# Reordering the pieces of the last tile in a row-wise infinity norm, and one tail store for two

## The chip, the cores and the metric

The kernel runs on one core of one Trainium2 chip. The metric is device time in microseconds; most executions agree within 0.3%. A trace's span runs from its first to its last instruction and is about 1.8 us shorter than the device time of the same execution.

## The reference

```python
x = np.random.randn(8192, 8192).astype(np.float32)     # 268 MB
out = np.linalg.norm(x, ord=np.inf, axis=1)            # max of |x| along each row
```

## The kernel before

Each of the 128 partitions handles 64 rows, two rows (16384 columns, 64 KB) to a tile, with three tile buffers. First come 24 bulk tiles, each one load of 8.39 MB and one VectorE reduce of 17.22 us. Then come 8 tail tiles, whose loads are cut into pieces (`TAIL`) so that VectorE can begin on a piece while the next one is still in flight. A maximum of each piece goes into `part`; one small reduce ("the merge") turns `part` into the results of the first 15 tail rows. The pieces of the last row are treated in another way: their partial maxima are written just behind the tile's data, so that the last reduce takes the last piece and all partial maxima in one instruction.

```python
TAIL = [
    [2944, 13440], [4096, 12288], [11520, 4864], [7680, 8704],
    [6528, 3328, 6528], [4864, 4096, 3328, 4096], [3968, 3584, 3328, 2944, 2560],
    [2432, 2176, 1920, 1664, 1536, 1280, 1152, 1024, 1152, 1024, 1024],
]                                     # reformatted: one list per tile
...
                if r < n_tail - 1:
                    absmax(part[:, r, k : k + 1], t[:, lo : lo + n])
                    if r == n_tail - 2 and k == count[r] - 1:
                        absmax(r_tail[:, : n_tail - 1], part[:])          # the merge
                        nc.scalar.dma_start(out=out_t[:, : n_tail - 1], ...)
                elif k < n_last - 1:
                    absmax(t[:, W + k : W + k + 1], t[:, lo : lo + n])
                else:
                    absmax(r_fin[:], t[:, lo : W + n_last - 1])           # the last reduce
    nc.sync.dma_start(out=out_t[:, n_tail - 1 :], in_=r_fin[:])
```

(Cuts are marked by dots. `absmax` is `reduce_max` with absolute values on VectorE; `nc.sync` and `nc.scalar` are the queues of SyncE, SP, and ScalarE, ACT.)

## Time and profile before

| | us |
|---|---|
| device time, median of 3 | 628.22 |
| span of the traced execution | 626.05 |
| last bulk load lands | 466.66 |
| last load of all lands | 622.90 |
| last reduce | 623.11 to 624.34 |
| last store | 624.37 to 625.78 |

How to read it: the last three rows follow one another. From the start of the last reduce on, nothing overlaps, so the reduce and the store count in full. Landings are read as the issue time of a load plus its time to landing.

Page of the kernel before: engine busy time with its share of the span, and the DMA queues with packets, MB and the share of the 16 DMA engines' time. q1 carries the loads, q10 the stores from ACT, q14 instruction fetches.

```profile
DVE 552.9 (88%) x64; POOL 0.2 (0%) x4
q1 hardware_dynamic: 8064, 268.44, 99.4%
q10 hardware_dynamic: 928, 0.03, 0.1%
q14 instruction: 2, 0.02, 0.0%
```

The load queue is busy all the time. VectorE (DVE) has 12% slack over the whole run, but that average hides the tail. The next view is the timeline of the kernel before from 605 us: start, duration, engine and line, with consecutive instructions of a kind merged.

```profile
603.36 11.64 DVE L139 TENSOR_REDUCE part<-t 128x1 f32<-128x2560 f32 x5
606.13 7.17 SPq L157 DMA_DIRECT2D t<-in_x_dram  x4
615.04 0.22 DVE L139 TENSOR_REDUCE r_tail<-part 128x15 f32<-128x60 f32 x1
615.17 7.91 DVE L139 TENSOR_REDUCE t<-t 128x1 f32<-128x1536 f32 x6
615.29 0.35 ACTq L169 DMA_DIRECT2D out_dram<-r_tail  x1
623.11 1.23 DVE L139 TENSOR_REDUCE r_fin<-t 128x1 f32<-128x1030 f32 x1
624.37 0.35 SPq L177 DMA_DIRECT2D out_dram<-r_fin  x1
```

The chain of waits of the same trace from 580 us: start, duration, what (pieces of 0.02 us left out).

```profile
556.05 40.57 DMA t<-in_x_dram
596.64 18.38 DVE part L139 x8
615.04 0.22 DVE r_tail L139
615.26 7.83 DVE t L139 x6
623.11 1.23 DVE r_fin L139
```

The chain leaves the loads at 596.6 us. From there to 624.34 us it stays on VectorE, which has no idle gap any more: the last landing at 622.90 is not on this chain at all, because VectorE was still 0.21 us behind when it came. The last load's own line among the DMA issues (KB, us from issue to landing; issued at 612.98) and the three stores' lines are:

```profile
t<-in_x_dram SPq DMA_DIRECT2D x1, 512.0 KB, 9.9
out_dram<-r_bulk ACTq DMA_DIRECT2D x1, 24.0 KB, 60.4
out_dram<-r_tail ACTq DMA_DIRECT2D x1, 7.5 KB, 5.4
out_dram<-r_fin SPq DMA_DIRECT2D x1, 0.5 KB, 1.4
```

### The profile page before, as it was taken

The numbers are of one execution on the slowest core, as the hardware profiler recorded it, in microseconds if no ns is written. First come the engines' busy times: TensorE is split into PE (matmuls) and PEld (weight loads), VectorE is DVE, ScalarE is ACT, GpSimd is POOL, SyncE is SP. The second block draws the span as 40 slices with busy tenths as digits, with TensorE's granted clock in tenths as the row PEclk, the third lists the DMA queues.
The fourth block names the chain that finished last, engine by engine and source line by source line (L and its number), as shares of the span: only waits on it lengthen the run. The fifth ranks groups of instructions, "written<-read, shape, count | busy, mean of one in ns | idle before, by whom it ended". The sixth has DMA issues, their size and how long they took to land.

```text
span 626.0 us, 199 instructions
## 1 busy us (share of the span) xinstructions
DVE 552.9 (88%) x64; POOL 0.2 (0%) x4
## 2 busy tenths in 40 slices
DVE  0588988889988889888898888988889999999998
POOL 0000000000000000000000000000000000000000
DMA  9999999999999999999999999999999999999997
GB/s 402 469 402 452 419 452 419 452 419 448 423 435 435 427 444 410 461 402 469 402 469 402 469 402 465 406 452 419 452 422 410 443 432 430 423 431 426 427 424 308
DMA packets 8994, 268.49 MB, mean 429 GB/s; under 512 B 1952, under 2 KB 1952, under 8 KB 3104
## 3 DMA queue, kind: packets, MB, share of 16 engines
q1 hardware_dynamic: 8064, 268.44, 99.4%
q10 hardware_dynamic: 928, 0.03, 0.1%
q14 instruction: 2, 0.02, 0.0%
HBM read 268.44 MB, written 0.03 MB: 429 GB/s over the span
## 4 chain that ended last, share of the span: by engine, by line
DMA 67%; DVE 29%; another core or an unknown queue 4%; SPq 0%; issue 0%
DMA t<-in_x_dram 67%; DVE r_bulk L139 22%; DVE part L139 5%; DVE t L139 1%; DVE r_fin L139 0%; SPq L157 0%; DVE r_tail L139 0%
## 5 line engine op out<-in xcount | busy, mean ns | idle before, releaser
L139 DVE TENSOR_REDUCE r_bulk<-t 128x2 f32<-128x16384 f32 x24 | 413.3, 17220 | 69.6 <-DMA t<-in_x_dram 69.6
L139 DVE TENSOR_REDUCE part<-t 128x1 f32<-128x8192 f32 (+18 forms) x31 | 130.4, 4274 | 0.8 <-DMA t<-in_x_dram 0.6
L139 DVE TENSOR_REDUCE t<-t 128x1 f32<-128x1152 f32 (+3 forms) x6 | 7.9, 1387 | 0.0
L139 DVE TENSOR_REDUCE r_fin<-t 128x1 f32<-128x1030 f32 x1 | 1.2, 1227 | 0.0
L136 DVE MEMSET part<- 128x60 f32 x1 | 0.1, 108 | 0.9 <-PEq L194 0.9
L139 DVE TENSOR_REDUCE r_tail<-part 128x15 f32<-128x60 f32 x1 | 0.2, 216 | 0.0
L194 POOL MEMSET const-uint8-127<- 128x1 uint8 x1 | 0.1, 102 | 0.0
L194 POOL MEMSET const-bfloat16-1.0<- 128x1 bf16 x1 | 0.1, 101 | 0.0
L194 POOL MEMSET const-float32-0.0<- 128x1 f32 x1 | 0.1, 98 | 0.2 <-issue 0.2
L194 POOL MEMSET const-float32-1.0<- 128x1 f32 x1 | 0.1, 98 | 0.0
## 6 DMA issues: line engine op xcount, KB each, us to landing
t<-in_x_dram SPq DMA_DIRECT2D x1, 6720.0 KB, 40.4
t<-in_x_dram SPq DMA_DIRECT2D x2, 3264.0 KB, 26.2
t<-in_x_dram SPq DMA_DIRECT2D x3, 2048.0 KB, 28.7
t<-in_x_dram SPq DMA_DIRECT2D x1, 6144.0 KB, 40.6
t<-in_x_dram SPq DMA_DIRECT2D x1, 5760.0 KB, 35.3
t<-in_x_dram SPq DMA_DIRECT2D x3, 1664.0 KB, 32.2
t<-in_x_dram SPq DMA_DIRECT2D x2, 2432.0 KB, 32.4
t<-in_x_dram SPq DMA_DIRECT2D x1, 4352.0 KB, 43.0
```

The source lines that it names most:

```text
L136: nc.vector.memset(part[:], 0.0)
L139: nc.vector.reduce_max(out=o, in_=i, axis=X, apply_absolute_value=True)
L194: nc = _bacc.Bacc("TRN2", target_bir_lowering=False, num_devices=1)
```

## The change

Its intent: shorten what follows the last landing. Both rows of the last tile now keep their partial maxima in the tile, each beside its last piece; the two last pieces are the last two loads, of 640 columns each. The merge of the other 14 rows needs nothing of the last tile any more, and one store writes all 16 tail rows. The other tail lists are cut anew.

```diff
 TAIL = [
-    [2944, 13440], [4096, 12288], [11520, 4864], [7680, 8704],
-    [6528, 3328, 6528], [4864, 4096, 3328, 4096], [3968, 3584, 3328, 2944, 2560],
-    [2432, 2176, 1920, 1664, 1536, 1280, 1152, 1024, 1152, 1024, 1024],
+    [9728, 6656], [5632, 10752], [9600, 6784], [9344, 7040],
+    [6784, 6528, 3072], [4736, 3072, 4224, 4352], [3968, 2432, 3072, 2944, 1792, 2176],
 ]
+LAST = (
+    [(0, w) for w in (2176, 2048, 1664, 1664)]
+    + [(1, w) for w in (1536, 1280, 1152, 1024, 896, 896, 768)]
+    + [(0, 640), (1, 640)]
+)
...
+    for j, (b, w) in enumerate(LAST):
+        final = left[b] == 0
+        to = slot[b] - w if final else at          # the last pieces go next to the partial maxima
+        frm = b * cols + col[b]
+        nc.sync.dma_start(out=t[:, to : to + w], in_=x_t[len(TAIL)][:, frm : frm + w])
+        if final:
+            absmax(r_tail[:, r : r + 1], t[:, to : slot[b] + parts_of[b]])
+        else:
+            absmax(t[:, k : k + 1], t[:, to : to + w])
+        if j == 0:
+            absmax(r_tail[:, : n_tail - B], part[:])
-    nc.sync.dma_start(out=out_t[:, n_tail - 1 :], in_=r_fin[:])
+    nc.sync.dma_start(out=out_t, in_=r_tail[:])
```

More of the change, by code (lines that the diff above doesn't have):

```diff
@@ L17 @@
 TAIL = [
-    [2944, 13440],
-    [4096, 12288],
-    [11520, 4864],
-    [7680, 8704],
-    [6528, 3328, 6528],
-    [4864, 4096, 3328, 4096],
-    [3968, 3584, 3328, 2944, 2560],
-    [2432, 2176, 1920, 1664, 1536, 1280, 1152, 1024, 1152, 1024, 1024],
-]
+    [9728, 6656],
+    [5632, 10752],
+    [9600, 6784],
+    [9344, 7040],
+    [6784, 6528, 3072],
+    [4736, 3072, 4224, 4352],
+    [3968, 2432, 3072, 2944, 1792, 2176],
+]
+LAST = (
[3 more added lines that the diff above has]
+)
 def segments(loads, cols):
@@ L107 @@
     W = B * cols
-    n_tail = B * len(TAIL)
+    n_tail = B * (len(TAIL) + 1)
     n_bulk_rows = rows // P - n_tail
@@ L123 @@
     segs = [segments(loads, cols) for loads in TAIL]
-    count = {}
-    for i, s in enumerate(segs):
-        for _, r, _, _ in s:
-            count[i * B + r] = count.get(i * B + r, 0) + 1
-    n_last = count[n_tail - 1]
-    k_max = max(count[r] for r in range(n_tail - 1))
-    assert n_last - 1 <= PAD
+    k_max = max(sum(r == b for _, r, _, _ in s) for s in segs for b in range(B))
+    parts_of = [sum(r == b for r, _ in LAST) - 1 for b in range(B)]
+    assert sum(parts_of) <= PAD
     r_bulk = outp.tile([P, A, G * B], F32)
     r_tail = outp.tile([P, n_tail], F32)
-    r_fin = outp.tile([P, 1], F32)
-    part = outp.tile([P, n_tail - 1, k_max], F32)
+    part = outp.tile([P, n_tail - B, k_max], F32)
     nc.vector.memset(part[:], 0.0)
@@ L149 @@
     nc.scalar.dma_start(out=out_b, in_=r_bulk[:])
-    seen = {}
     for i, loads in enumerate(TAIL):
@@ L154 @@
         todo = segs[i]
+        seen = [0] * B
         at = 0
@@ L159 @@
             for _, b, c, n in [s for s in todo if s[0] == j]:
-                r = i * B + b
-                k = seen.get(r, 0)
-                seen[r] = k + 1
-                lo = b * cols + c
-                if r < n_tail - 1:
-                    absmax(part[:, r, k : k + 1], t[:, lo : lo + n])
-                    if r == n_tail - 2 and k == count[r] - 1:
-                        absmax(r_tail[:, : n_tail - 1], part[:])
-                        nc.scalar.dma_start(
-                            out=out_t[:, : n_tail - 1], in_=r_tail[:, : n_tail - 1]
-                        )
-                elif k < n_last - 1:
-                    absmax(t[:, W + k : W + k + 1], t[:, lo : lo + n])
-                else:
-                    absmax(r_fin[:], t[:, lo : W + n_last - 1])
-    nc.sync.dma_start(out=out_t[:, n_tail - 1 :], in_=r_fin[:])
+                k, lo = seen[b], b * cols + c
+                absmax(part[:, i * B + b, k : k + 1], t[:, lo : lo + n])
+                seen[b] += 1
+    t = sbuf.tile([P, W + PAD], F32, tag="t")
+    left = parts_of[:]
+    col = [0] * B
+    at, slot = 0, {}
+    ends = [w for _, w in LAST[-B:]]
+    lo = W - sum(ends)
+    for b in range(B):
+        slot[b] = lo + ends[b]
+        lo = slot[b] + parts_of[b]
+    for j, (b, w) in enumerate(LAST):
[3 more added lines that the diff above has]
+        nc.sync.dma_start(out=t[:, to : to + w], in_=x_t[len(TAIL)][:, frm : frm + w])
+        col[b] += w
+        if final:
+            r = n_tail - B + b
+            absmax(r_tail[:, r : r + 1], t[:, to : slot[b] + parts_of[b]])
+        else:
+            left[b] -= 1
+            k = slot[b] + left[b]
+            absmax(t[:, k : k + 1], t[:, to : to + w])
+            at += w
+        if j == 0:
+            absmax(r_tail[:, : n_tail - B], part[:])
+    nc.sync.dma_start(out=out_t, in_=r_tail[:])
     nc.at_finalize(start_first_load_early)
```

## The prediction

> **What bounds the kernel now.** The load stream. The page gives q1 (the SP loads) 99.4% of the 16 DMA engines' span at 429 GB/s; successive landings give 19.34 us per 8.39 MB bulk tile, 434 GB/s. The Trainium skill ("DMA: Bandwidth & Descriptors", Specifications) gives 435 GB/s as the fabric ceiling; the trace agrees, so 268 MB cannot stream faster. VectorE is 88% busy, but starts the tail 17 us behind (bulk reduce of 17.22 us ending at 483.90) and catches up only at the end: in the timeline it works without a break of over 0.7 us from 483.8 to 624.34. The skill ("VectorE: DVE Perf Modes") says that the reduce has only its 1x mode; the trace agrees (8192 elements in 8.68 us, 1.04 ns each plus 0.14 us, of which 0.085 us overlaps the next one).
>
> Only the end is open to this change: the last load lands at 622.90, VectorE finishes the reduce before at 623.08, the final 1030-element reduce runs 623.11 to 624.34 (1.23 us), the 0.5 KB store 624.37 to 625.78, and the span ends at 626.05.
>
> **What changes.**
> - The last load and reduce shrink from 1024/1030 to 640/647 elements: about 0.82 us (the trace's 640-element form). Saves 0.40 us on the path.
> - The final reduce no longer depends on the reduce just before it: the 0.03 us hand-over becomes a 0.085 us overlap, and VectorE's lag behind the last landing, 0.21 us now, should be 0.05 to 0.1. Saves 0.1 us.
> - Loads in the tail: 31 to 34. From the intervals between landings I estimate 1.16 ns per column plus 0.065 us per load plus 0.04 us per further 2048 columns; this reproduces all 31 landings within 0.5 us cumulated. The new lists cost 0.28 us more.
> - The 7.5 KB ACT store amid the last loads (5.4 us to landing, 144 packets between the loads' packets; those loads take some 0.1 us more than the estimate) is gone. Saves 0.1 us.
> - The last store grows from 4 to 64 bytes per partition: packets of 60 bytes took 11 ns, of 4 bytes 9 ns, eight per engine. Costs 0.02 us.
> - Reduces in the tail: 39 to 42, each 0.06 us of overhead, 0.18 us. VectorE's idle time absorbs it. Stepping through the new list with these durations, it stays 0.02 to 0.25 us behind each landing in the last tile.
> - The reordered larger pieces move work about but save nothing: VectorE frees each buffer while over a tile is still in flight.
>
> **Sum.** The last load lands 0.2 us later (623.1), the last reduce ends 0.3 us earlier (about 624.0), and the store takes the same 1.4 us. I predict 627.9 us, 0.05% below 628.22; range 627.4 to 628.4. Faster by over 2%: 0.005; within 2%: 0.99; slower: 0.005.
>
> **What would show it.** Timeline: last reduce about 0.82 us, starting within 0.1 us of the last landing; last landing near 623.1; no ACT store after the bulk one; 64-byte store landing in about 1.4 us; q1 still above 99%.
>
> **What would make it wrong.** Two 8 KB instruction fetches share the DMA engines (one falls on a landing that is 0.3 us late); a third, or another placing, moves the end by 0.3 us. A destination at a 16-byte offset could slow the last load's writes. If the SP queue issues the small loads late, the stream starves. VectorE has almost no slack: an unforeseen wait of 0.3 us in the middle of the tail would appear in full.

## The result and the profile after

The median was 627.98 us (627.73 to 628.23, 6 runs) against 628.23 us before (628.11 to 629.08, 6 runs of the same comparison). The ratio was 0.9993, with a 95% interval of 0.9981 to 1.0006. Ratios here are the mean time of one kernel's fast runs over that of the other's in the same rounds, so they are not quite the ratios of the medians. By the 2% criterion the two are the same, and that interval alone can't tell the difference from zero.

The page of the kernel after, the lines that answer to those of before:

```profile
DVE 552.9 (88%) x67; POOL 0.2 (0%) x4
q1 hardware_dynamic: 8496, 268.45, 99.4%
q10 hardware_dynamic: 784, 0.02, 0.1%
q14 instruction: 2, 0.02, 0.0%
```

Its timeline from 604 us:

```profile
604.17 2.41 DVE L140 TENSOR_REDUCE part<-t 128x1 f32<-128x2176 f32 x1
606.48 8.55 SPq L179 DMA_DIRECT2D t<-in_x_dram  x5
606.61 0.21 DVE L140 TENSOR_REDUCE r_tail<-part 128x14 f32<-128x56 f32 x1
606.74 16.47 DVE L140 TENSOR_REDUCE t<-t 128x1 f32<-128x2176 f32 x11
623.13 1.55 DVE L140 TENSOR_REDUCE r_tail<-t 128x1 f32<-128x644 f32 x2
624.71 0.35 SPq L192 DMA_DIRECT2D out_dram<-r_tail  x1
```

The chain of waits of the kernel after, from 580 us (from 622.83 us on, where the last two reduces overlap, the view goes over to small pieces under other names; these are left out, as are pieces of 0.02 us):

```profile
553.77 35.14 DMA t<-in_x_dram
588.93 17.66 DVE part L140 x7
606.61 0.21 DVE r_tail L140
606.82 16.01 DVE t L140 x11
```

The last load (issued at 614.70) and the last store among the DMA issues, and, by form, the last reduce (the 1.23 us of the one before stand in its timeline above):

```profile
t<-in_x_dram SPq DMA_DIRECT2D x1, 320.0 KB, 8.9
out_dram<-r_tail SPq DMA_DIRECT2D x1, 8.0 KB, 1.4
```

```profile
L140 DVE TENSOR_REDUCE r_tail<-t 128x1 f32<-128x647 f32 x1 | 0.8, 816 | 0.0
```

The merge has moved from 615.0 to 606.6 us. The ACT store is gone from the end. The last reduce takes 0.82 us instead of 1.23, and the store of 8 KB takes 1.4 us like the one of 0.5 KB. But this one execution ended its span 0.35 us later than the traced one of before: its last bulk load had landed 0.31 us later (466.97), and its last load landed 156.64 us after that one, against 156.24 before. A single trace of each kernel therefore can't say what was won. What I need is a quantity that scatters less than the landings do. That quantity is the time from the last landing to the end of the last reduce: 1.44 us before, 1.07 us after.

### The profile page after: what moved, and what is told of

Read it like the earlier page. It is cut to its first block, busy times and chain, and to the rows that moved or that the text cites. A ratio compares the mean times of both kernels' runs of the same rounds, so it can differ in the third digit from the quotient of the medians.

```text
span 626.4 us, 204 instructions
## 1 busy us (share of the span) xinstructions
DVE 552.9 (88%) x67; POOL 0.2 (0%) x4
## 3 DMA queue, kind: packets, MB, share of 16 engines
q1 hardware_dynamic: 8496, 268.45, 99.4%
## 4 chain that ended last, share of the span: by engine, by line
DMA 63%; DVE 35%; issue 1%; another core or an unknown queue 0%; DVEq 0%
DMA t<-in_x_dram 63%; DVE r_bulk L140 24%; DVE part L140 8%; DVE t L140 3%; DVEq L220 0%; DVE r_tail L140 0%
## 5 line engine op out<-in xcount | busy, mean ns | idle before, releaser
L140 DVE TENSOR_REDUCE part<-t 128x1 f32<-128x8192 f32 (+20 forms) x28 | 121.6, 4410 | 0.9 <-DMA t<-in_x_dram 0.8
L140 DVE TENSOR_REDUCE t<-t 128x1 f32<-128x1664 f32 (+8 forms) x11 | 16.5, 1572 | 0.0
L140 DVE TENSOR_REDUCE r_tail<-t 128x1 f32<-128x644 f32 (+1 forms) x2 | 1.5, 814 | 0.0
```

Of the source, the lines that this page charges most:

```text
L140: nc.vector.reduce_max(out=o, in_=i, axis=X, apply_absolute_value=True)
```

## The experiments

Twelve kernels ran in three groups, each group on another chip and beside its own runs of the kernel before: e1 to e4 (kernel before: median 628.36, 9 runs), e5, e6, e7 and e9 (628.13, 9 runs), e8, e10, e11 and e12 (628.12, 9 runs). Each experiment has five timed runs and one trace. "Lag" is the time from the last landing to the start of the last reduce; "lag + last" is the time from the last landing to its end.

| kernel | last load after last bulk load, us | lag | last reduce | lag + last | median of time, us | ratio, 95% interval |
|---|---|---|---|---|---|---|
| before | 156.24 | 0.21 | 1.23 | 1.44 | 628.22 | |
| e9 before again | 156.34 | 0.21 | 1.23 | 1.43 | 628.27 | 1.0002 (0.9990, 1.0015) |
| after | 156.64 | 0.25 | 0.82 | 1.07 | 627.98 | 0.9993 (0.9981, 1.0006) |
| e1 after again | 156.13 | 0.24 | 0.82 | 1.05 | 627.89 | 0.9993 (0.9981, 1.0006) |
| e12 after, third | 156.49 | 0.25 | 0.81 | 1.07 | 627.79 | 0.9992 (0.9978, 1.0005) |
| e2 large pieces only | 156.15 | 0.22 | 1.23 | 1.44 | 628.12 | 0.9999 (0.9987, 1.0012) |
| e3 mid store | 156.46 | 0.19 | 0.82 | 1.01 | 627.92 | 0.9995 (0.9983, 1.0008) |
| e4 skip one reduce | 156.68 | 0.12 | 0.82 | 0.94 | 627.96 | 0.9992 (0.9979, 1.0006) |
| e5 small end, old order | 156.43 | 0.65 | 0.83 | 1.48 | 628.10 | 1.0001 (0.9989, 1.0014) |
| e10 e5 with early merge | 156.54 | 0.46 | 0.83 | 1.28 | 627.98 | 0.9997 (0.9984, 1.0009) |
| e6 coarse end | 156.35 | 0.09 | 2.29 | 2.38 | 629.00 | 1.0016 (1.0002, 1.0030) |
| e8 finer end | 156.48 | 0.53 | 0.55 | 1.09 | 627.92 | 0.9995 (0.9983, 1.0008) |
| e7 aligned end | 156.35 | 0.28 | 0.82 | 1.10 | 627.98 | 0.9996 (0.9984, 1.0009) |
| e11 two tiles | 156.61 | 0.16 | 0.81 | 0.98 | 627.78 | 0.9993 (0.9980, 1.0005) |

(The last bulk load's landing is taken as 0.02 us before the start of the reduce that waited for it.)

### Is there a gain at all? (e1, e9, e12)

The edit: none. e1 and e12 are the kernel after, e9 the kernel before.

> The changed kernel unaltered, for its scatter and a second trace. Theory A (the gain is real and comes from the smaller last reduce): 0.2 to 0.4 us under the kernel before in the mean, last reduce about 0.82 us, last load landing 156.5 us after the last bulk load (before: 156.24, first trace of the change: 156.64). Rival N (no gain, only scatter between runs): within 0.1 us of the kernel before.

> The kernel before, unaltered, for a second trace. Theory A: last landing to end of last reduce 1.44 us again, within 0.05; last landing 156.0 to 156.6 us after the last bulk landing, scatter from the place of the 8 KB instruction fetch. Rival N: this interval scatters as much as the totals do (some 0.5 us).

> The changed kernel unaltered beside the three others on this chip. Last landing to end of last reduce 1.07 us again, within 0.05; mean 0.2 to 0.4 us under the kernel before.

Lag + last came out at 1.05 and 1.07 us again, and at 1.43 us for the kernel before: it repeats within 0.02 us. The landing of the last load does not repeat: 156.13, 156.49 and 156.64 us in three traces of one and the same kernel. Over all groups, the 16 timed runs of the kernel after have a mean of 627.89 us and the 38 of the kernel before (with e9's five) 628.27 us. The difference is 0.39 us; from the scatter of these runs I work out a 95% interval of about 0.14 us to either side. It was 0.41, 0.45 and 0.49 us in the three comparisons taken separately. So the gain is real, though the interval of each single comparison includes no change at all, and it is 0.06%. A few long runs of the kernel before (up to 629.08 us) raise its mean: the medians of the two sets, 628.14 and 627.84 us, differ by 0.30 us.

The two traces e1 and after also show where much of the scatter arises. Both have one packet of the instruction queue q14 (8 KB) at 582.1 to 582.2 us. In both, the load of 4352 columns then lands: 5.25 us after its predecessor in e1, 5.71 us in the other. The neighbouring sizes suggest about 5.2 us (5.05 us was measured for 4224 columns). The timeline of VectorE alone around that time, first of the kernel after, then of e1:

```profile
570.97 12.85 DVE L140 TENSOR_REDUCE part<-t 128x1 f32<-128x4736 f32 x4
584.17 9.04 DVE L140 TENSOR_REDUCE part<-t 128x1 f32<-128x4352 f32 x2 [0.36 <-DMA t<-in_x_dram]
```

```profile
570.97 21.72 DVE L140 TENSOR_REDUCE part<-t 128x1 f32<-128x4736 f32 x6
```

In the kernel after VectorE waited 0.36 us for that landing, in e1 it did not wait. In six traces with these tail lists (after, e1, e3, e4, e7, e12) this interval was 5.71, 5.25, 5.57, 5.76, 5.50 and 5.62 us, so it differs by up to 0.5 us between runs of nearly the same program (5.34, 5.68 and 5.58 us in e2, e6 and e8, which share these lists). It holds nearly all the scatter of the last landing: without it, the three traces of the change have 150.93, 150.88 and 150.87 us from the last bulk landing to the last one.

The old lists have such a late load too, 4096 columns, in 5.18 us (before) and 5.28 us (e9). In e10, below, the packet comes later, and there this load takes 4.89 us. With 4.89 us for it in the kernel before, and 5.2 us for the 4352 columns in the change, the last load lands 155.95 and 155.96 us after the last bulk load before, and 156.13, 156.08 and 156.07 us in the change: 0.14 us later.

That the instruction packet is the cause is inferred. What speaks for it is that in e10 and e11, where the packet came at 610.1 and 606.9 us, the late load moved with it. But each trace has a second such packet, and the load around that one was never more than 0.1 us late, so a packet alone doesn't explain it.

### Do the larger pieces carry it? (e2)

```diff
 # the kernel before
-    [2944, 13440], ..., [3968, 3584, 3328, 2944, 2560],
+    [9728, 6656], ..., [3968, 2432, 3072, 2944, 1792, 2176],
     [2432, 2176, 1920, ..., 1152, 1024, 1024],
```

> The kernel before with the seven new larger tail lists; its last tile and its two tail stores are as before. Theory A (the gain comes from the last tile alone): no gain, the same as before or up to 0.2 us slower (one load and two reduces more). Rival B (the new larger pieces let VectorE catch up earlier and carry the gain): 0.2 us or more faster than before.

It is as slow as the kernel before (ratio 0.9999), with lag + last 1.44 us. The new lists for the seven earlier tiles gain nothing by themselves. In this trace VectorE waited 0.22 us for the first load of the last tile (at 606.2 us), and its lag at the end was 0.22 us all the same: what the earlier lists do doesn't reach the end of the old last tile.

### Does the removed store carry it? (e3)

```diff
 # the kernel after
             absmax(r_tail[:, : n_tail - B], part[:])
+            nc.scalar.dma_start(out=out_t[:, : n_tail - B], in_=r_tail[:, : n_tail - B])
-    nc.sync.dma_start(out=out_t, in_=r_tail[:])
+    nc.sync.dma_start(out=out_t[:, n_tail - B :], in_=r_tail[:, n_tail - B :])
```

> The changed kernel with the store of the 14 finished tail rows put back on the ACT queue amid the last loads, and the last store for two rows only. Theory A: the 144 small packets delay the last landing by about 0.1 us, so 0 to 0.1 us slower than the change, still under the kernel before. Rival C (the removed store is the gain): as slow as the kernel before, 0.25 us above the change.

Its median was 627.92 us, 0.03 us from e1's, and the last load landed 156.46 us after the last bulk load, amid the three traces of the change (156.13 to 156.64). The store amid the loads costs nothing that these runs resolve. Without the one late load (above) it is 150.89 us, against 150.87 to 150.93: no cost within 0.05 us. This still doesn't refute my 0.1 us, because e3 issues the store at 606.4 us, 9 us earlier than the kernel before does. In the one trace of e3 the last store took 1.72 us instead of 1.41 to 1.45; I can't say why.

### Is it just the smaller last piece? (e5)

This is the experiment that decides most. It makes the last reduce as small as the change does, with one line, and leaves everything else as before.

```diff
 # the kernel before
-    [2432, 2176, 1920, 1664, 1536, 1280, 1152, 1024, 1152, 1024, 1024],
+    [2432, 2176, 1920, 1664, 1536, 1280, 1152, 1024, 896, 896, 768, 640],
```

> The kernel before with one line changed: its last list ends 896, 896, 768, 640 in place of 1152, 1024, 1024, so the last reduce has 647 elements; row order, tail stores and all other lists as before. Theory A (the size of the last piece is the gain): from the last landing to the end of the last reduce 1.05 us as in the change (before: 1.44), last landing about 0.07 us later than before for one more load, total as fast as the change, 0.3 us under before. Rival R (the row order with both rows ending in the last two loads, or the single store, is needed): no faster than before.

It is not faster than the kernel before: ratio 1.0001. Lag + last was 1.48 us. The timeline of e5 from 615 us, and its last load (issued at 614.95) among the issues:

```profile
615.21 0.22 DVE L139 TENSOR_REDUCE r_tail<-part 128x15 f32<-128x60 f32 x1
615.34 8.37 DVE L139 TENSOR_REDUCE t<-t 128x1 f32<-128x1536 f32 x7
...
623.74 0.83 DVE L139 TENSOR_REDUCE r_fin<-t 128x1 f32<-128x647 f32 x1
```

```profile
t<-in_x_dram SPq DMA_DIRECT2D x1, 320.0 KB, 8.1
```

The last reduce takes 0.83 us as hoped. But it starts 0.65 us after its data landed (623.09), because VectorE is still at work on the pieces before. What the last reduce no longer does, VectorE has to do just before it, plus the overhead of one instruction more. Its chain of waits is that of the kernel before, on VectorE alone from 596.8 us. When an engine is behind, the end is the time of its last wait plus all its work since, and cutting that work into other pieces does not shorten it. So theory A, in the form in which I had written it for e5, is wrong: the small end alone is not enough, and rival R is right that something else of the change is needed. R's other half, the single store, is ruled out by e3, which keeps two stores and the whole gain in lag + last. The earlier lists are no candidate either: in e5 and in the kernel before, the first reduce of the last tile (606.31 and 606.14 us) starts 0.02 us after its landing, so the whole lag arises within that tile (see also e2). What is left is the last tile itself: its order, the sizes of its pieces and the place of the merge. No run separates these three; other sizes in the old order were not tried.

### What the new order buys (e10)

If e5 fails for VectorE's backlog, then taking work out of its last stretch must help. e10 is e5 with the merge before the last tile. The result is wrong (row 14's maximum isn't there yet), as the old order doesn't allow it.

```diff
 # e5
-                    if r == n_tail - 2 and k == count[r] - 1:
+                    if r == n_tail - 3 and k == count[r] - 1:
```

> Wrong result on purpose (row 14 of 16 is merged before its maxima are there): the small end in the old row order, e5, with the merge of partial maxima and its store moved from before the 1536-column piece (615 us) to before the last tile (606 us). In e5 the lag was 0.65 us and ate the whole gain. Theory B (what the new row order buys is an early merge, out of VectorE's last stretch): lag 0.35 to 0.4 us, last reduce 0.83 us, total 0.25 us under e5 and as fast as the change. Rival R2 (the lag in e5 has another cause, such as the hand-over to the last reduce): lag 0.55 us or more, total as e5.

The timeline of e10 from 606 us:

```profile
606.10 0.21 DVE L139 TENSOR_REDUCE r_tail<-part 128x15 f32<-128x60 f32 x1
...
611.53 3.95 DVE L139 TENSOR_REDUCE part<-t 128x1 f32<-128x1920 f32 x2 [0.17 <-DMA t<-in_x_dram]
615.39 8.37 DVE L139 TENSOR_REDUCE t<-t 128x1 f32<-128x1536 f32 x7
623.79 0.83 DVE L139 TENSOR_REDUCE r_fin<-t 128x1 f32<-128x647 f32 x1
```

The lag fell from 0.65 to 0.46 us, between my two figures. But the trace doesn't show that the early merge did it. The load for which VectorE waited 0.17 us at 611.5 us, 1920 columns, landed 2.85 us after its predecessor, against 2.28 us in e5 and in the kernel before: it was 0.57 us late, and an instruction packet came at 610.1 us, as the DMA view of e10 from 610 to 610.2 us shows:

```profile
q14 instruction: 1, 0.01, 9.7%
```

A late load lets VectorE catch up, wherever the merge is. Had this one come in time, its reduce would have started 0.25 us earlier, right behind the one before it, and it and all later loads would have landed 0.57 us earlier. The lag would then have been about 0.78 us (an estimate from this trace), no less than in e5. That is also what the rule above asks for: from about 606 us on VectorE has no wait in e5, so a merge at 606.1 us adds as much to its work after the last wait as one at 615.2 us. So e10 decides neither for theory B nor for R2.

What the traces do show is the hand-over. In before, e9, e2, e5 and e10 the last reduce needs the result of the reduce just before it and starts 0.03 us after that one ends. In the change it depends on older ones and starts 0.08 us before the other ends (623.86 against 623.94): 0.11 us in all, of the 0.40 us between e5 (0.65) and the change (0.25). Another part can be read off the sizes: the last two pieces of the change are equal, and from the first of them to the second the lag falls from 0.35 to 0.25 us. The rest is not isolated. The times (mean 628.06 us for e10, 628.19 for e5, of different groups) decide nothing.

### The trade along the taper (e6, e8, e4)

e6 ends in pieces of 2048 columns, e8 in pieces of 384; e4 takes 2.0 us of VectorE work out of the tile before the last (wrong: 1792 columns of one row in 64 aren't looked at, though the check of the result passed).

```diff
 # e6: the kernel after
+LAST = [(0, w) for w in (2176, 2048, 1920)] + [(1, w) for w in (1664, 1536, 1536, 1408)] + [(0, 2048), (1, 2048)]
 # e8: the kernel after
+LAST = [(0, w) for w in (2176, 2048, 1920, 1664)]
+    + [(1, w) for w in (1408, 1280, 1152, 1024, 896, 768, 640, 640)] + [(0, 384), (1, 384)]
 # e4: the kernel after
-                absmax(part[:, i * B + b, k : k + 1], t[:, lo : lo + n])
+                if not (i == 6 and j == 4):
+                    absmax(part[:, i * B + b, k : k + 1], t[:, lo : lo + n])
```

> The changed kernel with a coarser last tile: 9 loads in place of 13, the last two of 2048 columns each. Theory A: the last reduce takes 2.28 us instead of 0.82, the last load lands 0.2 to 0.3 us earlier for four loads fewer, VectorE no longer lags (0.02 us instead of 0.25), sum 1.0 us slower than the change (about 628.9). Rival V (VectorE's total work from the tile before the last sets the end): four reduces fewer save 0.24 us, so faster than the change.

> The changed kernel with a finer last tile: 14 loads in place of 13, the last two of 384 columns. Theory B (VectorE's backlog and the last reduce trade against each other, and the change sits on the flat of that trade): last reduce 0.55 us instead of 0.82, but VectorE's lag behind the last landing rises from 0.25 to 0.5 us, so total within 0.15 us of the change. Theory A in its simple form (the end is the last landing plus the last reduce): 0.2 us faster than the change.

> Wrong result on purpose: the changed kernel without the 2.0 us reduce of the 1792-column load in the tile before the last, so VectorE has 2 us of slack just before the end. Theory L (the end follows the last landing): the lag between the last landing and the last reduce falls from 0.25 us to 0.02 us, so at most 0.2 us faster, and not the 2 us taken away. Rival V (VectorE's own backlog sets the end): about 2 us faster. If VectorE's lag of 0.25 us was an accident of that one trace, no gain at all.

The timeline of e6 from 606.3 us, without the store:

```profile
606.36 13.42 DVE L140 TENSOR_REDUCE t<-t 128x1 f32<-128x2176 f32 x7
620.67 2.29 DVE L140 TENSOR_REDUCE r_tail<-t 128x1 f32<-128x2051 f32 x1 [0.89 <-DMA t<-in_x_dram]
623.15 2.29 DVE L140 TENSOR_REDUCE r_tail<-t 128x1 f32<-128x2052 f32 x1 [0.20 <-DMA t<-in_x_dram]
```

With the coarse end VectorE waits for the loads, the lag is down to 0.09 us, and the last reduce counts in full: lag + last 2.38 us, total 629.00 us (628.9 expected), the only experiment whose interval excludes the kernel before. Rival V is refuted there. With the finer end the last reduce is down to 0.55 us, as this line by form shows, and the lag is up to 0.53 us:

```profile
L140 DVE TENSOR_REDUCE r_tail<-t 128x1 f32<-128x392 f32 x1 | 0.6, 550 | 0.0
```

Lag + last is 1.09 us, the same as the change's 1.07. The change thus sits on the flat floor of this trade. In e4 VectorE waited 1.60 us before the 2176-column reduce that ends the tile before the last, as this line of its timeline shows:

```profile
603.78 2.42 DVE L140 TENSOR_REDUCE part<-t 128x1 f32<-128x2176 f32 x1 [1.60 <-DMA t<-in_x_dram]
```

So it entered the last tile without backlog; still the lag was 0.12 us at the end, not 0.02 as I had expected, and nothing came of it in the total (median 627.96 against 627.89 us in the same group). The lag of the change is for half the backlog that the last tile itself builds up: its late pieces shrink faster than VectorE gains on the loads. The other half VectorE brings with it: in the change it starts the first piece of the last tile 0.28 us after its landing (606.74 against 606.46), of which the merge just before takes 0.25 us. In e4 the wait hides it. So the merge, early as it is, still costs the change something at the end.

### The 16-byte offset (e7)

The last load's destination starts 16 bytes past a multiple of 64. e7 puts row 1's partial maxima ahead of the data, so that it starts at a multiple.

```diff
 # the kernel after
-        to = slot[b] - w if final else at
+        to = (slot[0] - w if b == 0 else slot[1] + parts_of[1]) if final else at
```

(The slots and the last reduce follow suit.)

> The changed kernel with row 1's partial maxima just ahead of its last piece, so that the last load's destination starts at a multiple of 64 bytes instead of 16 bytes past one. In four traces the last 640-column load took 0.81 to 0.83 us after the load before it, and the equal load before it 0.75 to 0.81. If the offset costs: the last interval falls to 0.78, total 0.05 us less. If it does not [...]: 0.81 to 0.83 again.

The last load landed 0.80 us after the one before, between my two figures (0.78, and 0.81 to 0.83 in the unaligned kernels). If the offset costs anything, it is at most 0.03 us, and nothing shows in the total: median 627.98 us, that of the change.

### An attempt to go further (e11)

```diff
 # the kernel after
-TAIL: 7 lists, LAST: 1 tile
+TAIL = [[9728, 6656], [5632, 10752], [9600, 6784], [8704, 7680], [6528, 6528, 3328], [3968, 3968, 4480, 3968]]
+FUSED = [both_end_last([3840, 2176, 2176], [2048, 2048, 2048, 2048]),
+         both_end_last([2176, 2048, 1664, 1536, 768], [1536, 1280, 1024, 1024, 1024, 896, 768, 640])]
+    absmax(r_tail[:, :n_plain], part[:])     # before the last two tiles
+    for i, loads in enumerate(FUSED, len(TAIL)): ...   # the loop of the change, for each
```

> An attempt to beat both: the last two tiles, not one, are loaded so that both rows end in their last two loads with their partial maxima beside them; the merge covers 12 rows and comes two tiles before the end; sizes chosen again with the measured intervals. Theory B: VectorE's lag at the last landing falls from 0.25 us to 0.1 to 0.15, same last reduce, last landing 0 to 0.2 us earlier; total 0.15 to 0.4 us under the change (627.6 to 627.8). If VectorE's lag was not what is left to gain: as the change.

The lag fell to 0.16 us and lag + last to 0.98 us, the lowest of all correct kernels. The total did not follow: median 627.78 us, and 627.79 for the change in the same group. Its timeline from 605 us shows one reason in this trace:

```profile
605.67 2.42 DVE L147 TENSOR_REDUCE t<-t 128x1 f32<-128x2176 f32 x1 [0.20 <-DMA t<-in_x_dram]
608.59 14.03 DVE L147 TENSOR_REDUCE t<-t 128x1 f32<-128x2048 f32 x10 [0.50 <-DMA t<-in_x_dram]
```

An instruction packet came at 606.9 us, in the last tile, and the load of 2048 columns landed 2.92 us after its predecessor, 0.49 us more than the 2.43 us of the other traces. (VectorE waited 0.50 us for it, as long as it was late, so unlike in e10 the low lag doesn't come from it.) I don't claim e11 as a gain.

## Why the prediction was right or wrong

The total was right: 627.9 predicted, 627.98 measured, and 627.89 in the mean of all 16 runs. The gain of 0.3 us forecast against 0.39 us (within about 0.14) measured is right in size as well. But the range given, 627.4 to 628.4 us, holds the old time too, so the total says little about the mechanism, and that it came within 0.1 us is luck in part: the steps came out unevenly.

- **The load stream bounds the kernel**: right. q1 stood at 99.4% before and after. The Trainium skill's 435 GB/s ("DMA: Bandwidth & Descriptors", Specifications) against the 434 GB/s of the bulk tiles leaves nothing to gain there.
- **The last reduce, 0.40 us**: right in size (1.23 to 0.82 us). Wrong as a cause on its own. The prediction counted it as saved "on the path" in full; e5 made the same reduction without the rest of the change and gained nothing, as the lag grew by 0.44 us. The saving holds only because the new last tile keeps the lag where it was. Of the 0.40 us of lag between e5 and the change the hand-over is 0.11 us; how the order, the sizes and the place of the merge share the rest is open.
- **"VectorE's lag behind the last landing, 0.21 us now, should be 0.05 to 0.1. Saves 0.1 us"**: this step failed. The lag was 0.25, 0.24 and 0.25 us in three traces, and my own test, a start within 0.1 us of the last landing, was not met. The hand-over did change as forecast (0.03 us after to 0.08 us before), but VectorE was further behind. What failed is the pace of the loads: my formula makes the last 12 intervals between landings 0.11 us longer in sum than the trace of the change has them, so that VectorE seemed to catch up. Stepped through again with the merge in full, the last tile gives a lag of 0.09 to 0.10 us with the formula's intervals and 0.20 to 0.21 us with the measured ones (an estimate).
- **More loads, 0.28 us later**, less 0.1 us for the store: right in sum. The last landing was 156.29 us after the last bulk one in the mean of two traces before, and 156.42 us in three of the change. The scatter of 0.5 us is larger than this difference, but nearly all of it is the one late load; with that at its time on schedule, the change lands 0.14 us later (see "Is there a gain at all?"). The two terms were not separated.
- **The larger pieces save nothing**: right (e2).
- **The 64-byte store**: right, 1.42 to 1.43 us against 1.41 to 1.42.
- **Instruction fetches as the main risk**: right in kind. A load near one of the two packets was up to 0.57 us late, and by how much differs from run to run; that the packet does it is inferred.
- **The skill's statement that the reduce has only a 1x mode** ("VectorE: DVE Perf Modes", the perf-mode tier table): the durations agree in all forms, from 550 ns for 392 elements to 2.29 us for 2052, 1.04 to 1.05 ns per element more.

The 0.3 us was thus a sum of a term counted right, a saving of 0.1 us that did not come, and costs of about the right size. From the traces the sum is -0.41 (last reduce) + 0.04 (lag) + 0.13 (landing) + 0.01 (store) = -0.23 us; the totals say -0.39 (by medians -0.30). The difference is about the uncertainty of the totals and stays open. (The sum leaves out the time up to the last bulk landing, which the change doesn't touch; it was 466.66 to 466.97 us.)

## What to carry to other kernels

When the producer and the consumer of a stream run at nearly the same rate, ask which engine the chain of waits is on just before the end. If it is the consumer, and it has had no wait for a long time, a smaller last piece only moves work ahead of it (e5); what counts is all its work since its last wait, with the hand-overs in it. Before an edit gets the credit for a shorter lag, look whether a load came late in that trace: a late producer lets the consumer catch up (e10). And where totals scatter by more than the effect, look for an interval inside the trace that doesn't scatter: here lag + last repeated within 0.02 us while the totals moved by 0.5 us.

## What the Trainium skill lacked or had wrong

- "Runtime: NRT & Kernel Launch", Instruction fetch mechanics, calls the cost of a page crossing "one DMA tail-bump, mostly hidden". In a kernel that the loads bound it may not be hidden: near one 8 KB packet of q14 a load came 0.05 to 0.57 us late (5.25 to 5.76 us for 4352 columns where about 5.2 was due; 2.92 us instead of 2.43 for 2048 columns in e11; 2.85 us instead of 2.28 for 1920 columns in e10). Near the other packet of each trace it was 0.1 us at most. The cause is inferred from the place.
- "VectorE: DVE Perf Modes", The DRAIN you can't avoid, says that a semaphore after each op cost nothing extra there, in a row of copies. It gives no cost for an op that has to wait for the one just before it. Here a reduce that needs the one just before it starts 0.03 us after that one's recorded end, one that does not starts 0.08 us before it: 0.11 us for a dependent hand-over. (The same section says that an op which is not held starts earlier, which agrees.) The page's tier table gives the mode of the reduce but no time; the runs show 0.14 us plus 1.04 ns per element.
- "DMA: Bandwidth & Descriptors", Anatomy of one DMA (SWDGE path), gives about 2 us as the fixed cost of a single DMA on that path. The loads here are issued from SP and queued back to back, which the page gives no cost for; the runs show far less for one more of them: 0.81 us for 640 columns and 1.24 us for 1024, which is 0.05 and 0.03 us more than at the 1.18 ns per column of the bulk loads (19.34 us for 16384).
- No page says what a small store takes among loads: 1.41 to 1.45 us for 0.5 to 8 KB with the DMA engines idle (1.72 us once, for 1 KB in e3), 5.4 us for 7.5 KB amid the last loads, 60.4 us for 24 KB in pieces of 32 bytes behind large loads.
